# Sums over partitions of the adaLN vectors: VectorE block transposes and partials through DRAM in place of TensorE matmuls with a column of ones

## The chip, the cores and the metric

The kernel runs on one core of a Trainium2 chip. The metric is device time in microseconds (us) of that core, the median of several executions. All arithmetic is on float32 data; the large products are float32 split into a high and a low float32r part.

## The reference, cut to what matters

One encoder layer on x (1 x 1024 x 2048) with a conditioning vector c (1 x 2048). Everything that the change touches comes from the first line: a vector of 6144 sums over the 2048 rows of `w_ada`, cut into `shift`, `scale` and `gate`.

```python
mod = jax.nn.silu(c) @ w_ada + b_ada            # (1, 6144)
shift, scale, gate = jnp.split(mod, 3, axis=-1)
h = rmsnorm(x, pre_g) * (1.0 + scale[:, None]) + shift[:, None]
proj = h @ w_in                                  # q, k, v, gate_a, u, gate_p
...
g = jax.nn.sigmoid(h @ w_merge + b_merge)
merged = g_a * (y_a @ w_br_attn) + g_p * (y_p @ w_br_pool)
o = merged @ w_out
return x + gate[:, None] * rmsnorm(o, post_g)
```

`shift` and `scale` are wanted early for the first half of h's 2048 columns and later for the second half. `gate * post_g` is wanted only by the last stage, which multiplies every row of o with it.

## The kernel before, in words

The work is a chain of large products, each cut with Strassen's scheme (Winograd's form) into seven products (`product`, L233 to L238). One pair of output blocks is one call of `strassen`: seven products of 12 matmuls each (3 forms: high by high, high by low, low by high; 4 matmuls of 128x512 in each). TensorE works through these pairs with hardly a pause. For each product ScalarE makes the high part of the weights (`whi`, L96) and VectorE the low part (`wlo`, L97). Four buffers of each let them run ahead. VectorE also adds products that lie in PSUM to others (`u<-V,u`, L103), which frees the PSUM bank V of a pair for the next pair's product T3.

The modulation vector is made in three ways. The parts that are needed first (columns 0 to 3 of the first half) come from matmuls at the start of the program (`row_sums`, `modulation`). The late parts come from VectorE beside the first pass over the weights (`pass1`): `ada_sums(j)`, j = 4 to 7, and `gate_sum(kc, q)`, q = 0 and 1, each load rows of `w_ada` and accumulate them, weighted with silu(c), over the 16 groups of 128 rows into `accs[j]` (128x512) and `gacc[q]` (128x1024). What is then left is a sum over the 128 partitions. `sum_rows` does it by TensorE: the accumulator is the moving operand, and `onez` (128x32, a column of ones beside zeros) the weights; four such matmuls fill four groups of 32 rows of one PSUM bank.

- `late_rows` does it for the four `accs` (bank PMR, tile `msum`), `late_columns` turns the four rows into columns with four transposes on TensorE (bank PMT) and adds the bias into `modc`.
- `gate_row` does it for the two `gacc` (bank GATE), adds the bias, multiplies with post_g (both in `grow`, fetched by `gate_vectors` as rows), and stores 2048 numbers to `pg_d` in DRAM.

The order of this side work is written by hand. `units` holds 64 pairs of a load and a weighted sum; `unit_step(n)` runs load n and sum n - 3 (`AHEAD` = 3) and, by the table `then`, one further step ahead of sum m = n - 3. One `unit_step` comes after most products of a pair (`EASY`). Within an engine a layer below the kernel places the instructions by dependence; those in `keep(...)` stay in program order, and the others may be placed earlier. The loads and stores of the main work are on SP's queue, in order. GpSimd's queue (POOL) carries memsets that claim buffers, and a few DMAs.

At the start of the program, POOL fetches six small vectors (`rows`), then claims with one-column memsets the buffers `xT`, `B11h` and so on, which ScalarE and VectorE write before the first products (PB, L822). The first modulation columns are made at the same time: `GEMV` matmuls on eight tiles of `w_ada` that SP loads, the sums `PM`, and the first transposes of x (`XT`).

Of the kernel before, what the change touches and what calls it, by code (L numbers as in the profile page):

```python
# [21 lines left out]
P = 128  # L22
# [21 lines left out]
def encoder_layer(ctx: ExitStack, tc: tile.TileContext, x, c, table, w_ada, b_ada, pre_g,  # L44
# [32 lines left out]
    def uid(s):  # L77
        cnt[0] += 1
        return f"{s}_{cnt[0]}"

    def bank(tag, name="b"):
        return psum.tile([P, 512], F32, tag=tag, name=uid(name), bufs=1 if tag in SEEDED else 2)
# [8 lines left out]
    def keep(ins):  # L91

        return tc.keep_in_program_order(ins)
# [8 lines left out]
    def add(o, a, b, eng=None):  # L102
        return (eng or nc.vector).tensor_tensor(o, a, b, ALU.add)  # L103
# [30 lines left out]
    ws_d = {n: dram.tile([D // 2, D // 2], F32, name=f"ws_d{n}") for n in ("S1", "S2", "S3", "S4")}  # L134
    m_d = dram.tile([D, S], F32, name="m_d")
    pg_d = dram.tile([1, D], F32, name="pg_d")


    def put(op, name, j, src):
# [1011 lines left out]

        return load_, sum_

    onez = gp.tile([P, 32], F32, name="onez")
    nc.gpsimd.memset(onez, 0.0)
    nc.gpsimd.memset(onez[:, 0:1], 1.0)
    accs, gsum = {}, {}

    def bias_lines():
# [2 lines left out]

    def gate_vectors():

        gsum["v"] = t = xa.tile([P, 2, 512], F32, tag="xa", name=uid("grow"))
        nc.gpsimd.memset(t, 0.0)
        for k, src in enumerate((b_ada[0, 2 * D:3 * D], post_g[0])):
            for n in range(4):
                nc.gpsimd.dma_start(t[32 * n:32 * n + 1, k], src[n * 512:(n + 1) * 512].rearrange("(o n) -> o n", o=1))

    def sum_rows(name, srcs):

        ps = bank("at", name)
        for n, src in enumerate(srcs):
            nc.tensor.matmul(ps[32 * n:32 * n + 32, :], onez, src, start=True, stop=True, tile_position=(0, 32 * n))
        return ps

    def gate_row():
        t, g = (gsum["v"][:, k] for k in range(2))
        add(t, sum_rows("GATE", [gacc[q][:, n * 512:(n + 1) * 512] for q in range(2) for n in range(2)]), t)  # L1180
        nc.vector.tensor_tensor(t, t, g, ALU.mult)
        for k in range(4):
            nc.gpsimd.dma_start(pg_d[0:1, k * 512:(k + 1) * 512], t[32 * k:32 * k + 1, :])

    def late_rows():
        pm = sum_rows("PMR", [accs[j] for j in range(4, 8)])
        gsum["m"] = xa.tile([P, 1024], F32, tag="xa", name="msum")[:, 0:512]
        nc.scalar.activation(gsum["m"], pm, AF.Copy)

    def late_columns():  # L1190
        pt = bank("at", "PMT")
        for g in range(4):
            nc.tensor.transpose(pt[:, g * P:(g + 1) * P], gsum["m"][:, g * P:(g + 1) * P], ident)
        sums_ = pt.rearrange("p (g h j r) -> p g h j r", g=2, h=2, j=4)[:, :, :, :, 0]
        bias = cols[:, 16:48].rearrange("p (g j h) -> p g h j", g=2, h=2)[:, :, :, 4:8]
        for g in range(2):
            nc.vector.tensor_tensor(modc[:, g, :, 4:8], sums_[:, g], bias[:, g], ALU.add)
        nc.vector.scalar_tensor_tensor(
            modc[:, 1, :, 4:8], modc[:, 1, :, 4:8], 1.0,
            cols[:, 48:64].rearrange("p (j h) -> p h j", h=2)[:, :, 4:8], op0=ALU.add, op1=ALU.mult)  # L1200
# [3 lines left out]
    for j in range(4, 8):  # L1204
        units += ada_sums(j)
    nu = len(units)
    then = {nu: late_rows, nu + 2: late_columns, 6 - AHEAD: bias_lines, nu + 2 * KT - AHEAD: gate_vectors}
    units += [gate_sum(kc, q) for q in range(2) for kc in range(KT)]

    def unit_step(n):  # L1210
# [6 lines left out]
            units[n][0]()  # L1217

    side = deque(lambda n=n: unit_step(n) for n in range(len(units) + AHEAD))
    side.extend((lambda: None, gate_row))  # L1220
    EASY = ((0, 2, 4, 6), (0, 1, 3, 5, 6), (0, 2, 4, 6))
    n1 = PAIRS - RAMP - 9
    sums = deque(weight_sums(j, h_) for h_ in range(2) for j in range(KT // 2))
# [755 lines left out]
```

## Time and profile before

| | before |
|---|---|
| median of 3 runs | 2086.41 us (2085.77 to 2087.27) |
| the profiled execution | 2088.67 us, of which 2086.9 us are the span of the instructions |
| TensorE (PE) | 2070.1 us busy, 99% |
| VectorE (DVE) | 1556.7 us, 75% |
| ScalarE (ACT) | 1111.0 us, 53% |
| GpSimd (POOL) | 42.6 us, 2% |
| DMA | 476.62 MB, mean 228 GB/s |

Times in the profile count from the start of the span. A fp32 matmul is two passes in the records: the four matmuls of PMR are eight rows "x6" and "x2".

### The profile page before, as it was taken

The page shows a single profiled execution, that of the slowest core. Times are in us where ns is not written, and L with a number is a line of the kernel's source. Part 1 is how long each engine was busy: PE and PEld are TensorE (multiplying, and loading weights), DVE is VectorE, ACT ScalarE, POOL GpSimd, SP SyncE. Part 2 cuts the span into 40 slices and gives each one's busy share as a digit, 9 for nine tenths or more (in the row PEclk, how much of TensorE's full clock was granted, in tenths as well). Part 3 has the DMA queues.
Part 4 walks back from the last instruction along what each step waited for, and adds up shares of the span by engine and source line. Part 5 has one row for each costly group of instructions (what it writes and reads, how often), then busy time and mean ns, then how long its engine had stood idle before and what let it go on. Part 6 is the DMA issues. An engine that isn't in the chain of part 4 may idle for free.

```text
span 2086.9 us, 29056 instructions
## 1 busy us (share of the span) xinstructions
PE 2070.1 (99%) x9524; PEld 1702.2 (82%) x9524; DVE 1556.7 (75%) x2805; ACT 1111.0 (53%) x2121; POOL 42.6 (2%) x143
## 2 busy tenths in 40 slices
PE   8999999999999999999999999999999999999998
PEld 6678887888888888888888888888888788888886
DVE  5889677776565876777777688857867977889667
ACT  5764444444564634666665444334645644767554
POOL 1100000001000000000000000010000000000000
PEclk9999999999999999999999999999999999999999
DMA  9978877887675477645554576675754566786897
GB/s 343 355 270 267 282 240 245 282 284 223 198 232 170 156 250 258 208 164 174 182 170 149 186 233 222 208 239 187 232 175 158 176 201 202 225 305 207 297 334 247
DMA packets 303393, 476.62 MB, mean 228 GB/s; under 512 B 24322, under 2 KB 140650, under 8 KB 303240
## 3 DMA queue, kind: packets, MB, share of 16 engines
q1 hardware_dynamic: 297616, 459.89, 67.2%
q0 software_dynamic: 4560, 12.75, 1.6%
q10 hardware_dynamic: 1064, 2.11, 0.3%
q8 instruction: 75, 1.23, 0.3%
q14 instruction: 78, 0.64, 0.1%
HBM read 346.70 MB, written 130.05 MB: 228 GB/s over the span
## 4 chain that ended last, share of the span: by engine, by line
PE 91%; DMA 4%; DVE 3%; ACT 1%; issue 1%; SPq 0%; DVEq 0%; ACTq 0%; POOL 0%; POOLq 0%
PE Z L237 30%; PE V L237 20%; PE X L237 20%; PE Z L1686 2%; PE Z L1688 2%; PE Z L1687 2%; PE PB L822 1%; PE X L1686 1%; PE X L1687 1%; PE X L1688 1%; PE V L1687 1%; PE V L1686 1%; PE V L1688 1%; DMA raw<-in_w_in_dram 1%; PE PT L1396 1%
## 5 line engine op out<-in xcount | busy, mean ns | idle before, releaser
L96 ACT ACTIVATE whi<-raw 128x512 fp32r<-128x512 f32 (+1 forms) x528 | 314.7, 600 | 482.8 <-PE Z L237 235.2
L97 DVE TENSOR_TENSOR wlo<-raw,whi 128x512 fp32r<-128x512 f32 (+1 forms) x528 | 339.7, 649 | 144.5 <-PE Z L237 110.9
L97 DVE TENSOR_TENSOR wlo<-wr,whi 128x512 fp32r<-128x512 f32 x224 | 150.7, 689 | 51.5 <-ACT whi L96 46.0
L96 ACT ACTIVATE whi<-wr 128x512 fp32r<-128x512 f32 x224 | 138.2, 628 | 86.9 <-DVE wlo L97 29.8
L103 DVE TENSOR_TENSOR raw<-raw,raw 128x512 f32<-128x512 f32 x76 | 52.5, 690 | 92.7 <-DMA raw<-in_w_merge_dram 62.6
L96 ACT ACTIVATE whi<-ws 128x512 fp32r<-128x512 f32 (+1 forms) x88 | 53.0, 602 | 72.2 <-PE X L237 60.8
L237 PE MATMUL Z<-B22h,whi 128*128 128x512 f32 x328 | 89.9, 392 | 0.0
L237 PE MATMUL Z<-T2h,wlo 128*128 128x512 f32 x328 | 88.9, 390 | 0.8 <-DVE wlo L97 0.8
L237 PE MATMUL Z<-T1h,whi 128*128 128x512 f32 x328 | 89.6, 390 | 0.0
L237 PE MATMUL X<-B11h,whi 128*128 128x512 f32 x328 | 89.5, 391 | 0.0
L237 PE MATMUL X<-B21h,whi 128*128 128x512 f32 x328 | 89.5, 391 | 0.0
L237 PE MATMUL V<-T3h,whi 128*128 128x512 f32 x328 | 89.4, 391 | 0.0
L237 PE MATMUL V<-T4h,whi 128*128 128x512 f32 x328 | 89.3, 391 | 0.0
L237 PE MATMUL Z<-T2h,whi 128*128 128x512 f32 x328 | 89.0, 390 | 0.3 <-ACT Z L293 0.2
L237 PE MATMUL X<-B11l,whi 128*128 128x512 f32 x328 | 89.2, 390 | 0.0
L237 PE MATMUL Z<-T1l,whi 128*128 128x512 f32 x328 | 89.0, 390 | 0.0
L237 PE MATMUL Z<-B22l,whi 128*128 128x512 f32 x328 | 88.9, 390 | 0.0
L237 PE MATMUL V<-T3l,whi 128*128 128x512 f32 x328 | 88.9, 390 | 0.0
L237 PE MATMUL X<-B21l,whi 128*128 128x512 f32 x328 | 88.8, 390 | 0.0
L237 PE MATMUL V<-T4h,wlo 128*128 128x512 f32 x328 | 88.8, 390 | 0.0
L237 PE MATMUL X<-B11h,wlo 128*128 128x512 f32 x328 | 88.8, 390 | 0.0
L237 PE MATMUL V<-T4l,whi 128*128 128x512 f32 x328 | 88.8, 390 | 0.0
(421 smaller groups left out, 4908.7 us busy)
## 6 DMA issues: line engine op xcount, KB each, us to landing
part<-part_d SPq DMA_DIRECT2D x136, 256.0 KB, 5.0
ada<-in_w_ada_dram SPq DMA_DIRECT2D x128, 256.0 KB, 5.4
raw<-in_w_merge_dram SPq DMA_DIRECT2D x64, 512.0 KB, 5.4
wr<-ws_dS SPq DMA_DIRECT2D x60, 512.0 KB, 5.4
raw<-in_w_in_dram SPq DMA_DIRECT2D x56, 512.0 KB, 4.1
wr<-in_w_out_dram SPq DMA_DIRECT2D x48, 512.0 KB, 5.0
proj_d<-part SPq DMA_DIRECT2D x68, 256.0 KB, 2.3
sw<-in_w_out_dram SPq DMA_DIRECT2D x64, 256.0 KB, 4.9
```

What stands on the lines that cost most here:

```text
L96: ins = (nc.scalar.activation(hi, src, AF.Copy), nc.vector.tensor_tensor(lo, src, f32(hi), ALU.subtract))
L97: nc.vector.tensor_tensor(lo, src, f32(hi), ALU.subtract))
L103: return (eng or nc.vector).tensor_tensor(o, a, b, ALU.add)
L237: nc.tensor.matmul(ps, w_[:, i], op[mov][j][m_], start=fresh and i == 0 and n == 0, stop=i == nj - 1 and n == 2, skip_group_check=True)
L822: keep(nc.tensor.matmul(opened[i, blk], w[:, kh, nt * P:(nt + 1) * P], mov[kh][m], start=j == n == 0, stop=j == 1 and n == 5, skip_group_c ...
L1396: nc.tensor.transpose(pt[:, i * P:(i + 1) * P], p[:, i * P:(i + 1) * P], ident)
L1686: nc.tensor.matmul(pb, hi, w[0], start=first, stop=False, skip_group_check=True)
L1687: nc.tensor.matmul(pb, lo, w[0], start=False, stop=False, skip_group_check=True)
L1688: nc.tensor.matmul(pb, hi, w[1], start=False, stop=last, skip_group_check=True)
```

## The change

`sum_rows`, `late_rows` and `onez` go. Six calls of `fold` come: VectorE transposes an accumulator in blocks of 32x32, sums each block row over 32 numbers into a tile of 128x4x4 (or 128x4x8 for the gate), and a DMA on POOL's queue stores that to DRAM (`fold_d`). `fetch_folds` loads it back with four DMAs so that the four partials of one output lie in one partition, and `sum_folds` adds the four. `gate_row` now works on 128x16 columns; `gate_vectors` fetches b_ada and post_g in the same layout, number by number, into a tile of its own and without a memset, and the product goes to `pg_d` number by number in one DMA. `late_columns` comes two units later than before.

```diff
+    fold_d = {what: dram.tile([P, 64], F32, name=f"fold_{what}") for what in ("columns", "gate")}
...
-    onez = gp.tile([P, 32], F32, name="onez")
-    nc.gpsimd.memset(onez, 0.0)
-    nc.gpsimd.memset(onez[:, 0:1], 1.0)
...
     def gate_vectors():
 
-        gsum["v"] = t = xa.tile([P, 2, 512], F32, tag="xa", name=uid("grow"))
-        nc.gpsimd.memset(t, 0.0)
+        gsum["v"] = t = xa2.tile([P, 2, KT], F32, name="gate_vectors")
         for k, src in enumerate((b_ada[0, 2 * D:3 * D], post_g[0])):
-            for n in range(4):
-                nc.gpsimd.dma_start(t[32 * n:32 * n + 1, k], src[n * 512:(n + 1) * 512].rearrange("(o n) -> o n", o=1))
-
-    def sum_rows(name, srcs):
-
-        ps = bank("at", name)
-        for n, src in enumerate(srcs):
-            nc.tensor.matmul(ps[32 * n:32 * n + 32, :], onez, src, start=True, stop=True, tile_position=(0, 32 * n))
-        return ps
+            nc.gpsimd.dma_start(t[:, k], src.rearrange("(t n) -> n t", n=P))
+
+    def fold(what, src, t0):
+
+        w = src.shape[1]
+        nt = w // P
+        turned = xa.tile([P, 1024], F32, tag="xa", name=uid("turned"))[:, 0:w]
+        keep(nc.vector.transpose(turned, src))
+        r = xa2.tile([P, 4, 8], F32, tag="fold", name=uid("fold"), bufs=2)[:, :, 0:nt]
+        keep(nc.vector.tensor_reduce(r.rearrange("p u t -> p t u"), turned.rearrange("p (t u j) -> p t u j", u=4, j=32),
+                                     op=ALU.add, axis=AX.X))
+        nc.gpsimd.dma_start(fold_d[what].rearrange("p (u t) -> p u t", u=4)[:, :, t0:t0 + nt], r)
+
+    def fetch_folds(what):
+
+        gsum[what] = t = xa2.tile([P, 4, KT], F32, name=uid("folds"))
+        for u in range(4):
+            nc.gpsimd.dma_start(t[32 * u:32 * u + 32], fold_d[what].rearrange("(a i) c -> i a c", a=4)[:, :, u * KT:(u + 1) * KT])
+
+    def sum_folds(what):
+
+        t = xa2.tile([P, KT], F32, name=uid("sums"))
+        keep(nc.vector.tensor_reduce(t, gsum[what].rearrange("p a t -> p t a"), op=ALU.add, axis=AX.X))
+        return t
 
     def gate_row():
-        t, g = (gsum["v"][:, k] for k in range(2))
-        add(t, sum_rows("GATE", [gacc[q][:, n * 512:(n + 1) * 512] for q in range(2) for n in range(2)]), t)
+        t, (b, g) = sum_folds("gate"), (gsum["v"][:, k] for k in range(2))
+        add(t, t, b)
         nc.vector.tensor_tensor(t, t, g, ALU.mult)
-        for k in range(4):
-            nc.gpsimd.dma_start(pg_d[0:1, k * 512:(k + 1) * 512], t[32 * k:32 * k + 1, :])
-
-    def late_rows():
-        pm = sum_rows("PMR", [accs[j] for j in range(4, 8)])
-        gsum["m"] = xa.tile([P, 1024], F32, tag="xa", name="msum")[:, 0:512]
-        nc.scalar.activation(gsum["m"], pm, AF.Copy)
+        nc.gpsimd.dma_start(pg_d[0].rearrange("(t n) -> n t", n=P), t)
 
     def late_columns():
-        pt = bank("at", "PMT")
-        for g in range(4):
-            nc.tensor.transpose(pt[:, g * P:(g + 1) * P], gsum["m"][:, g * P:(g + 1) * P], ident)
-        sums_ = pt.rearrange("p (g h j r) -> p g h j r", g=2, h=2, j=4)[:, :, :, :, 0]
+        sums_ = sum_folds("columns").rearrange("p (j g h) -> p g h j", g=2, h=2)
...
-    then = {nu: late_rows, nu + 2: late_columns, 6 - AHEAD: bias_lines, nu + 2 * KT - AHEAD: gate_vectors}
+    then = {nu + 1: partial(fetch_folds, "columns"), nu + 4: late_columns, 6 - AHEAD: bias_lines,
+            nu + 2 * KT - AHEAD - 3: gate_vectors}
+    then.update({8 * (j - 3): lambda j=j: fold("columns", accs[j], 4 * (j - 4)) for j in range(4, 8)})
+    then[nu + KT] = lambda: fold("gate", gacc[0], 0)
...
-    side.extend((lambda: None, gate_row))
+    side.extend((lambda: fold("gate", gacc[1], 8), partial(fetch_folds, "gate"), lambda: None, gate_row))
```

On TensorE the order stays as it was, with the twelve instructions (8 matmuls with `onez`, 4 transposes) taken out. Three other places move.

POOL, at the start of the program, before the change: the memsets that claim buffers follow each other.

```order
L389 MEMSET shz 128x128
L398 MEMSET tab 33x8
L455 MEMSET rb 128x1
L435 MEMSET xT_187 128x1
L435 MEMSET xT_189 128x1
L435 MEMSET xT_191 128x1
```

POOL at the same place now:

```order
L390 MEMSET shz 128x128
L399 MEMSET tab 33x8
L456 MEMSET rb 128x1
L1165 DMA gate_vectors<-in_b_ada_dram 128x16x1
L1165 DMA gate_vectors<-in_post_norm_g_dram 128x16x1
L436 MEMSET xT_189 128x1
L436 MEMSET xT_191 128x1
```

The two element-by-element DMAs of `gate_vectors`, written for the end of `pass1`, have no wait and stand among the first instructions of POOL, ahead of all the memsets that claim xT, B11h and the rest.

DVE, behind the last weighted sum of `accs[7]`, before the change (`raw`, `ws` and `wlo` are the weights of the main products; `modc` the modulation columns; `gacc` the gate's accumulator; `u<-V,u` the addition that frees bank V):

```order
L106 TENSOR_TENSOR raw_3669<-raw_3669,raw_3667 128x4x128
L97 TENSOR_TENSOR wlo_3898<-raw_3669,whi_3897 128x512
L103 TENSOR_TENSOR raw_3839<-raw_3839,raw_3841 128x4x128
L97 TENSOR_TENSOR wlo_3916<-raw_3667,whi_3915 128x512
L97 TENSOR_TENSOR wlo_3942<-raw_3839,whi_3941 128x512
L106 TENSOR_TENSOR raw_3839<-raw_3839 128x4x128
L97 TENSOR_TENSOR wlo_3948<-ws_3945,whi_3947 128x512
L1197 TENSOR_TENSOR modc<-PMT_3886,cols 128x2x4 x2
L1198 SCALAR_TENSOR_TENSOR modc<-modc,cols 128x2x4
L612 SCALAR_TENSOR_TENSOR gacc_3798<-gada_3763,sc,gacc_3798 128x1024
L106 TENSOR_TENSOR ws_4110<-raw_4008 128x512
L103 TENSOR_TENSOR u_839_3864<-V_3767,u_839_3864 128x512
```

DVE at the same place now, from the reduction of the last block transpose on:

```order
L1174 TENSOR_REDUCE fold_3807<-turned_3805 128x4x4
L611 TENSOR_SCALAR gacc_3810<-gada_3707,sc 128x1024
L97 TENSOR_TENSOR wlo_3925<-raw_3681,whi_3924 128x512
L613 SCALAR_TENSOR_TENSOR gacc_3810<-gada_3749,sc,gacc_3810 128x1024
L103 TENSOR_TENSOR raw_3851<-raw_3851,raw_3853 128x4x128
L613 SCALAR_TENSOR_TENSOR gacc_3810<-gada_3777,sc,gacc_3810 128x1024
L97 TENSOR_TENSOR wlo_3951<-raw_3851,whi_3950 128x512
L106 TENSOR_TENSOR raw_3851<-raw_3851 128x4x128
L97 TENSOR_TENSOR wlo_3957<-ws_3954,whi_3956 128x512
L1187 TENSOR_REDUCE sums_3981<-folds_3855 128x16
L1200 TENSOR_TENSOR modc<-sums_3981,cols 128x2x4 x2
L1201 SCALAR_TENSOR_TENSOR modc<-modc,cols 128x2x4
```

The reduction `sums<-folds` stands in DVE's queue eight rows behind the fold whose way through DRAM it waits for; the addition `u<-V,u` of this pair is the very next row behind what is shown.

DVE at the end of the gate's sums, now (before the change the additions `grow<-GATE,grow` and the product stood at about this place):

```order
L1174 TENSOR_REDUCE fold_5050<-turned_5048 128x8x4
L97 TENSOR_TENSOR wlo_5104<-raw_4999,whi_5103 128x512
L103 TENSOR_TENSOR raw_4999<-raw_4999,raw_5001 128x4x128
L106 TENSOR_TENSOR raw_4999<-raw_4999 128x4x128
L97 TENSOR_TENSOR wlo_5110<-ws_5107,whi_5109 128x512
L106 TENSOR_TENSOR ws_5305<-raw_5164 128x512
L103 TENSOR_TENSOR u_1069_5022<-V_4941,u_1069_5022 128x512
L97 TENSOR_TENSOR wlo_5146<-raw_4844,whi_5145 128x512
L1187 TENSOR_REDUCE sums_5140<-folds_5095 128x16
L103 TENSOR_TENSOR sums_5140<-sums_5140,gate_vectors 128x16
L1193 TENSOR_TENSOR sums_5140<-sums_5140,gate_vectors 128x16
```

The same pattern: seven rows between the reduction that a DMA stores and the one that waits for the four loads.

## The prediction

> **What bounds the kernel now.** I read the page first, then the busy time by stage, then the order of time at the four places that the change touches. The page:
>
> ```profile
> span 2086.9 us, 29056 instructions
> PE 2070.1 (99%) x9524; PEld 1702.2 (82%) x9524; DVE 1556.7 (75%) x2805; ACT 1111.0 (53%) x2121; POOL 42.6 (2%) x143
> ...
> PE 91%; DMA 4%; DVE 3%; ACT 1%; issue 1%; SPq 0%; DVEq 0%; ACTq 0%; POOL 0%; POOLq 0%
> ...
> L237 PE MATMUL Z<-T2h,wlo 128*128 128x512 f32 x328 | 88.9, 390 | 0.8 <-DVE wlo L97 0.8
> ```
>
> TensorE is the bound: it is busy in 99% of the span and makes 91% of the chain. The last row says how far the others are behind it: in the whole run it waited 0.8 us for a low weight of VectorE. By stage (PE, weight loads, DVE, ACT, POOL, then the granted clock and the share of the DMA engines):
>
> ```profile
> 0.00:20.00 20.00, 14.63 (x72) 7.34 (x73) 6.61 (x15) 5.66 (x10) 4.92 (x38) 1.00 0.92 300
> 20.00:40.00 20.00, 19.47 (x120) 15.51 (x119) 13.71 (x33) 16.72 (x39) 0.00 (x0) 1.00 1.04 364
> 219.00:360.00 141.00, 140.77 (x621) 114.66 (x619) 107.42 (x165) 57.82 (x95) 0.00 (x0) 1.00 0.77 251
> 435.00:520.00 85.00, 85.00 (x379) 69.46 (x378) 61.52 (x85) 35.71 (x58) 6.72 (x13) 1.00 0.78 252
> ```
>
> Two things follow. In the stage with the side work (219 to 520) PE is full and DVE has a quarter to spare, so what leaves PE there is time won. In the first 20 us PE is busy 14.63 only, and the DMA engines are the full resource (0.92, then 1.04): what is added to them there is paid.
>
> **What leaves TensorE.** PE in order of time at the four places (start, length, tile, count):
>
> ```profile
> 353.10 1.07 PE L237 MATMUL X<-B11h,wlo 128*128 128x512 f32 x4
> 354.10 1.06 PE L1175 MATMUL PMR<-acc,onez 128*32 128x512 f32 x6
> ...
> 356.12 1.08 PE L237 MATMUL V<-T3l,whi 128*128 128x512 f32 x4
> ...
> 357.95 0.84 PE L237 MATMUL Z<-B22h,whi 128*128 128x512 f32 x3
> 359.01 1.05 PE L1175 MATMUL PMR<-acc,onez 128*32 128x512 f32 x2 [0.23 <-DVE acc L612]
> ...
> 361.25 1.07 PE L237 MATMUL Z<-B22h,wlo 128*128 128x512 f32 x4
> 362.17 1.07 PE L237 MATMUL Z<-T2h,whi 128*128 128x512 f32 x4
> ...
> 366.70 1.07 PE L237 MATMUL X<-B21h,wlo 128*128 128x512 f32 x4
> 367.61 0.60 PE L1193 MATMUL PMT<-ident,msum 128*128 128x128 f32 x4
> ...
> 368.98 1.08 PE L237 MATMUL V<-T4l,whi 128*128 128x512 f32 x4
> ```
>
> ```profile
> 506.11 1.07 PE L237 MATMUL Z<-T1h,wlo 128*128 128x512 f32 x4
> 507.10 1.06 PE L1175 MATMUL GATE<-gacc,onez 128*32 128x512 f32 x8
> ...
> 509.13 1.08 PE L237 MATMUL X<-B11l,whi 128*128 128x512 f32 x4
> ```
>
> The lengths overlap, so the price is read from starts. From 362.17 to 366.70 lie five groups of four: 0.906 us each. Two groups are 1.81 us; what is over between the rows above belongs to the removed work, its restart and its 0.23 us of waiting included. First PMR: 356.12 - 353.10 = 3.02, over 1.21. Second PMR: 361.25 - 357.95 = 3.30, over 1.49. PMT: 368.98 - 366.70 = 2.28, over 0.47. GATE: 509.13 - 506.11 = 3.02, over 1.21. The four matmuls of one bank fill four column groups side by side, which is why eight passes of about 600 ns cost little more than one. **Sum: 4.4 us off the path**, 0.21% of the kernel. That is the whole gain. The ACT copy into `msum` goes too; ACT is half idle, so it counts as nothing.
>
> **What is added to VectorE, and what hides it.** No row shows a block transpose. The nearest are a cast at 0.43 us and a two-operand instruction at 0.69 us for 128x512, and 1.28 us for 128x1024:
>
> ```profile
> 12.80 0.43 DVE L803 CAST whi<-wide 128x512 fp32r<-128x512 f32 x1
> 13.26 0.69 DVE L106 TENSOR_TENSOR wlo<-wide,whi 128x512 fp32r<-128x512 f32 x1
> L612 DVE SCALAR_TENSOR_TENSOR gacc<-gada,sc,gacc 128x1024 f32<-128x1024 f32 x30 | 38.4, 1280 | 1.7 <-DMA gada<-in_w_ada_dram 1.5
> ```
>
> I take 0.69 and 1.28 for transpose and reduction alike (one pass over one element stream; at twice that a transpose would be 1.4 and 2.6). Four column folds are 4 x 1.38 = 5.5 us, two gate folds 2 x 2.56 = 5.1; the two `grow` instructions (1.4) go. That is 9 us more, 5.5 of it in a stage with 33 us of idle DVE. DVE's idle time there is mostly waiting for PE to give `wlo` buffers back, so it runs ahead; I cost it at nothing. If it were not ahead, the most is one fold, 1.4 or 2.6 us, at each of six places.
>
> **The way through DRAM.** `sums<-folds` waits on DVE, with all of DVE's queue behind it, for: a store, four issues, a load. The prices:
>
> ```profile
> L1183 POOL DMA_DIRECT2D pg_d<-grow x4: 484/484/487, 510.2 to 511.6; - x4
> ...
> DMA to landing us min/median/max: 2.2/3.2/4.9
> 358.21 0.75 DVE L612 SCALAR_TENSOR_TENSOR acc<-ada,sc,acc 128x512 f32<-128x512 f32 x1
> 371.49 0.68 DVE L103 TENSOR_TENSOR u<-V,u 128x512 f32<-128x512 f32 x1
> 376.26 1.07 PE L237 MATMUL V<-T3h,whi 128*128 128x512 f32 x4
> 508.10 1.20 PE L237 MATMUL X<-B11h,whi 128*128 128x512 f32 x4
> ```
>
> *Columns.* The last weighted sum ends at 358.96. Transpose, one `wlo`, reduction: 361.0. Store 3.2, three issues of 0.48 ahead of the last load, load 3.2: 368.9 (366.9 with the fastest landings, 372.3 with the slowest). Seven rows of DVE work lie between, so DVE waits about a microsecond, up to 4. Behind it comes `u<-V,u`, done 1.3 us after the landing: 370.2, at most 373.6. PE wants bank V for its next T3 product at 376.26, less the 3.2 us that PMR and PMT took: 373.1. So it fits by 3 us, and misses by 0.5 at worst; I take 0.2. *Gate.* The same way ends 8 us after its reduction. DVE waits some 3 us there, but the next `wlo` behind it is for the product T2, whose last third starts eleven groups (10 us) behind the row at 508.10: covered.
>
> **What is added at the start.** The order shows the two `gate_vectors` DMAs as the first work of POOL behind `rb`. Each moves 2048 single numbers.
>
> ```profile
> 4.75 0.12 POOL L455 MEMSET rb<- 128x1 f32 x1
> 4.98 0.12 POOL L657 MEMSET B11h<- 128x1 f32 x1
> 8.13 0.38 SPq L761 DMA_DIRECT2D wide<-in_w_in_dram  x1
> 10.20 1.03 PE L528 MATMUL GEMV<-ada,scz 128*32 128x256 f32 x8
> 13.00 0.69 ACT L684 ACTIVATE B11h<-XT,modc 128x512 fp32r<-128x512 f32 x1 [1.34 <-PE XT L491]
> PEld GEMV L528 <- DMA ada<-in_w_ada_dram: 4.7, 6, 1.2
> ...
> L381 POOL DMA_DIRECT2D rows<-in_pre_norm_g_dram x1: 492/492/492, 3.1 to 3.1; - x1
> L837 POOL DMA_DIRECT2D ramp_d<-c x8: 539/539/579, 49.8 to 74.7; - x8
> ...
> q0 software_dynamic: 256, 0.02, 1.2%
> ```
>
> *POOL's time.* An issue of 16 rows took 492 ns, one of 128 rows 539: 0.42 ns for a row more. Carried on to 2048 it is 1.35 us for each DMA, 2.7 for both. The memset of B11h moves from 4.98 to 7.7; ACT writes B11h at 13.0. Nothing is lost as long as one issue takes less than 4 us.
>
> *The DMA engines' time.* The last row is POOL's queue in the 14 us from 476 to 490: 256 packets (half of them 128 bytes, half semaphore writes) took 1.2% of 16 engines, 10.5 ns each. 4096 numbers at that price are 43 us of engine time, 2.7 us on each of 16. Below, the packets could fall in gaps (0). The loads that they meet are the tail of the `ada` tiles, for which GEMV waits six times, then x, then `wide`, issued at 8.13 and cast at 12.80 for the first product. All of it is just in time, and the engines are full, so most of it is paid: I take 2.0 us. Nothing behind gives it back, since PE is full from 20 us on.
>
> Here the Trainium skill speaks against the change: "DMA: Bandwidth & Descriptors", rules for kernel authors, says that a strided last dimension becomes one descriptor per element and should be rearranged. "VectorE: DVE Perf Modes", the three transpose paths, puts such an element-wise copy at 19 times a 1309 ns transfer of 128x128; that is an estimate of 1.5 ns per element, 6.2 us for 4096, and by it the sum would be 2088.4. No row of this trace shows such a copy.
>
> The other small DMAs (2048 numbers of `pg_d`, six stores of 512 short runs, eight loads of 128) come at 300 us and later, where the DMA engines have a fifth free and nobody waits; nothing.
>
> **The sum.** -4.4 (PE) + 2.0 (start) + 0.2 (bank V) = -2.2 us. The profiled execution has a span of 2086.9 and a time of 2088.67, 2.3 above the median of 2086.41; the terms are differences, so I apply them to the median: **2084.2 us**. 0.2%, 4.2 us, is about what a measurement here can tell from no change, so this is "the same", slightly below.
>
> **Rivals.**
> - *The start is free.* The numbers slip in between the loads. For: POOL's six small DMAs ahead of them do. Against: the DMA share of 0.92 and the six waits of GEMV. Time: 2086.4 - 4.4 = 2082.0, faster.
> - *POOL is slow at making 2048 descriptors.* Then the memsets are late and the first products with them. It decides from 4 us per issue on; beyond it the start slips by twice the excess. At 8 us the start is 8 us late: 2086.4 - 4.4 + 8 + 2 = 2092, slower. For: no DMA here has over 128 rows, so the slope is carried on 16-fold. Against: the slope itself.
> - *A number costs the DMA engines far more than a short row.* In the window from 1 to 13 us the hardware queue's packets, mostly 1 KB rows, took 52 ns each:
>
> ```profile
> q1 hardware_dynamic: 3329, 3.45, 89.6%
> ```
>
>   That bounds it above: 13.2 us on each engine, 2095. Half-way in ratio, 23 ns, it is 6.0 us and 2088.2. The skill's 19 times comes to the same place.
> - *The way through DRAM holds PE.* If landings take 5 us and more under load, bank V is late by 1 to 3 us: 2085 to 2087.
>
> **How the numbers follow.** Forecast 0.50; start free 0.18; POOL slow 0.13; dear numbers 0.11; DRAM way 0.08. Faster by over 0.2% (below 2082.2): the second case and a little of the first, 0.20. Slower (above 2090.6): POOL slow, and a third of the dear numbers, 0.17. The same: 0.63. The range runs from 2081.6, the full gain with the spread of the runs, to 2089.5, which takes in the half-way price of the numbers and leaves out slow POOL and the upper bound.
>
> **What would show it.** PE loses L1175 and L1193, and its starts around them close up. DVE gets nine microseconds more busy time and two waits for `folds` of 1 to 4 us, with no wait of PE for bank V behind. The two L1165 issues take about 1.35 us each; the first product PB starts at 15.5 to 16 in place of 13.74. The prediction is wrong if PB starts at 13.8 (then 2082), or if B11h waits for POOL.

## The result and the profile after

The changed kernel takes 2098.22 us, the median of 6 runs (2096.37 to 2099.54); the kernel before took 2086.84 beside it (2085.70 to 2090.41). The ratio is 1.0047, 95% interval 1.0036 to 1.0058: 10 us slower by the ratio, 11.4 by the two medians, and outside the forecast range of 2081.6 to 2089.5. The profiled executions say the same, 2097.8 us of span against 2086.9.

The page of the changed kernel; its lines are numbered one higher than before in `product` (L238 for L237):

```profile
span 2097.8 us, 29039 instructions
PE 2069.1 (99%) x9504; PEld 1701.9 (81%) x9504; DVE 1563.4 (75%) x2819; ACT 1111.1 (53%) x2120; POOL 48.0 (2%) x145
...
PE 85%; DMA 6%; DVE 4%; issue 3%; ACT 1%; SPq 0%; POOL 0%; DVEq 0%; ACTq 0%; POOLq 0%
...
L238 PE MATMUL V<-T3h,whi 128*128 128x512 f32 x328 | 89.8, 393 | 6.3 <-DVE u L103 6.3
L238 PE MATMUL Z<-T2h,wlo 128*128 128x512 f32 x328 | 89.1, 391 | 3.8 <-DVE wlo L97 3.8
```

TensorE's share of the chain fell from 91% to 85%, and in the last two rows stands what it now waits for: 6.3 us for `u` and 3.8 us for low weights, where the largest such entry before was 0.8. By stage (the columns as in the prediction):

```profile
0.00:20.00 20.00, 12.58 (x58) 6.12 (x59) 4.64 (x12) 3.79 (x7) 7.31 (x40) 0.91 0.95 260
360.00:390.00 30.00, 28.28 (x125) 23.06 (x125) 19.54 (x30) 12.22 (x20) 2.93 (x5) 1.00 0.81 257
435.00:470.00 35.00, 32.17 (x141) 25.97 (x140) 27.87 (x37) 14.16 (x23) 0.72 (x1) 1.00 0.84 273
500.00:520.00 20.00, 18.25 (x81) 14.80 (x80) 12.86 (x18) 7.36 (x12) 2.32 (x4) 1.00 0.70 223
520.00:540.00 20.00, 18.56 (x82) 14.90 (x81) 8.17 (x15) 7.10 (x13) 1.79 (x3) 1.00 0.63 69
```

Before, PE was full (30.00, 35.00, 20.00, 20.00) in the last four. The places are these, in order of time (PE rows with the wait ahead of them in brackets):

```profile
378.26 1.20 PE L238 MATMUL V<-T3h,whi 128*128 128x512 f32 x4 [1.72 <-DVE u L103]
...
437.12 1.20 PE L238 MATMUL V<-T3h,whi 128*128 128x512 f32 x4 [1.22 <-DVE u L103]
...
458.06 1.21 PE L238 MATMUL V<-T3h,whi 128*128 128x512 f32 x4 [1.61 <-DVE u L103]
...
517.27 1.19 PE L238 MATMUL V<-T3h,whi 128*128 128x512 f32 x4 [1.75 <-DVE u L103]
...
526.26 1.20 PE L238 MATMUL Z<-T2h,wlo 128*128 128x512 f32 x4 [1.44 <-DVE wlo L97]
...
546.92 1.19 PE L238 MATMUL Z<-T2h,wlo 128*128 128x512 f32 x4 [1.23 <-DVE wlo L97]
...
596.77 1.20 PE L238 MATMUL Z<-T1h,whi 128*128 128x512 f32 x4 [0.58 <-ACT u L252]
...
600.43 1.20 PE L238 MATMUL X<-B11h,whi 128*128 128x512 f32 x4 [0.62 <-ACT c L333]
```

To see what each costs, every matmul of one trace is set beside the same matmul of the other and the starts are subtracted. The changed kernel runs 3.3 us late at 60 us of the time before, 0.1 at 371 (so PMR and PMT did give 3.2), 3.7 at 440, 5.6 at 475, 8.2 at 520, 11.5 at 620, and 10.6 at the end. That is the ledger which the experiments have to explain.

*The columns' way through DRAM* (POOL rows are DMA issues; the bracket is what the engine waited for):

```profile
362.49 0.68 DVE L1174 TENSOR_REDUCE fold<-turned 128x16 f32<-128x512 f32 x1
363.46 0.71 POOL L1176 DMA_DIRECT2D fold_columns<-fold  x1 [37.97 <-DVE fold L1174]
370.88 2.22 POOL L1182 DMA_DIRECT2D folds<-fold_columns  x4 [6.71 <-DMA fold_columns<-fold]
376.86 0.26 DVE L1187 TENSOR_REDUCE sums<-folds 128x16 f32<-128x64 f32 x1 [7.52 <-DMA folds<-fold_columns]
377.52 0.68 DVE L103 TENSOR_TENSOR u<-V,u 128x512 f32<-128x512 f32 x1
378.23 0.33 SPq L338 DMA_DIRECT2D part_d<-u  x1
378.83 0.38 SPq L188 DMA_DIRECT2D raw<-in_w_merge_dram  x1
```

From the end of the reduction (363.2) to the sums it took 13.7 us; DVE stood 7.52 us, `u` came late, and with it SP: its next load of `raw` stands behind the store of `u` in the same queue. *The gate's store* writes 2048 single numbers, each a run of four bytes by itself. What it does is seen in the DMA throughput of 520 to 540 us (one figure per half microsecond) and in the landings (KB each, median us):

```profile
GB/s 225 258 328 326 119 78 62 16 0 0 0 0 0 0 0 6 64 345 50 16 1 1 13 8 17 26 43 41 61 29 25 29 8 25 20 8 51 109 139 201
...
raw<-in_w_merge_dram SPq DMA_DIRECT2D x2, 512.0 KB, 14.6
...
pg_d<-sums POOLq DMA_DIRECT2D x1, 8.0 KB, 13.0
```

The store of 2048 numbers is issued at 525.90. From 529 to 538.5 the DMA engines move 1 to 61 GB/s, with two loads of half a megabyte waiting; those land after 14.6 us. In the same stretch before, `raw` landed in 5.0 us.

### The profile page after: what moved, and what is told of

Its sections match the earlier page's. It is cut to its first block, busy times and chain, and to the rows that moved or that the text cites. A ratio compares the mean times of both kernels' runs of the same rounds, so it can differ in the third digit from the quotient of the medians.

```text
span 2097.8 us, 29039 instructions
## 1 busy us (share of the span) xinstructions
PE 2069.1 (99%) x9504; PEld 1701.9 (81%) x9504; DVE 1563.4 (75%) x2819; ACT 1111.1 (53%) x2120; POOL 48.0 (2%) x145
## 3 DMA queue, kind: packets, MB, share of 16 engines
q8 instruction: 74, 1.21, 0.2%
## 4 chain that ended last, share of the span: by engine, by line
PE 85%; DMA 6%; DVE 4%; issue 3%; ACT 1%; SPq 0%; POOL 0%; DVEq 0%; ACTq 0%; POOLq 0%
PE Z L238 27%; PE X L238 18%; PE V L238 18%; PE Z L1692 2%; PE Z L1693 2%; PE Z L1694 2%; PE PB L823 2%; DMA raw<-in_w_merge_dram 2%; PE X L1692 1%; PE V L1692 1%; PE V L1693 1%; PE X L1693 1%; PE V L1694 1%; PE X L1694 1%; PE PT L1402 1%
## 5 line engine op out<-in xcount | busy, mean ns | idle before, releaser
L106 DVE TENSOR_TENSOR ws<-raw 128x512 f32<-128x512 f32 (+1 forms) x88 | 57.5, 653 | 55.1 <-DMA raw<-in_w_merge_dram 42.3
L238 PE MATMUL V<-T3h,whi 128*128 128x512 f32 x328 | 89.8, 393 | 6.3 <-DVE u L103 6.3
L238 PE MATMUL Z<-T2h,wlo 128*128 128x512 f32 x328 | 89.1, 391 | 3.8 <-DVE wlo L97 3.8
L238 PE MATMUL Z<-T1h,whi 128*128 128x512 f32 x328 | 89.7, 390 | 0.6 <-ACT u L252 0.6
L238 PE MATMUL X<-B11h,whi 128*128 128x512 f32 x328 | 89.5, 391 | 0.6 <-ACT c L333 0.6
L238 PE MATMUL Z<-B22h,whi 128*128 128x512 f32 x328 | 89.6, 392 | 0.0
L238 PE MATMUL X<-B21h,whi 128*128 128x512 f32 x328 | 89.5, 391 | 0.0
L238 PE MATMUL Z<-T2h,whi 128*128 128x512 f32 x328 | 89.0, 390 | 0.3 <-ACT Z L294 0.2
L238 PE MATMUL X<-B11l,whi 128*128 128x512 f32 x328 | 89.3, 390 | 0.0
L238 PE MATMUL V<-T4h,whi 128*128 128x512 f32 x328 | 89.2, 391 | 0.0
L238 PE MATMUL Z<-B22l,whi 128*128 128x512 f32 x328 | 88.9, 390 | 0.0
L238 PE MATMUL V<-T3l,whi 128*128 128x512 f32 x328 | 88.9, 390 | 0.0
L238 PE MATMUL Z<-T1l,whi 128*128 128x512 f32 x328 | 88.9, 389 | 0.0
L238 PE MATMUL X<-B21l,whi 128*128 128x512 f32 x328 | 88.9, 390 | 0.0
L238 PE MATMUL X<-B11h,wlo 128*128 128x512 f32 x328 | 88.8, 390 | 0.0
L238 PE MATMUL V<-T4h,wlo 128*128 128x512 f32 x328 | 88.8, 390 | 0.0
```

Of the source, the lines that this page charges most:

```text
L106: return nc.vector.tensor_tensor(o, a, b, ALU.subtract)
L238: nc.tensor.matmul(ps, w_[:, i], op[mov][j][m_], start=fresh and i == 0 and n == 0, stop=i == nj - 1 and n == 2, skip_group_check=True)
```

## The experiments

All ratios are to runs of the kernel before on the same chip. The lateness is that of the same matmul against the trace of before, in us, at six times of before and at the end; it is worked out as above from one profiled execution each (median over seven neighbours). Steps of up to 1.6 us stand also where nothing was changed: f4 is the kernel before up to 511 us, and it goes from -0.5 at 60 to 1.1 at 371.

| kernel | ratio, 95% interval | 60 | 371 | 440 | 475 | 520 | 620 | 2075 |
|---|---|---|---|---|---|---|---|---|
| changed | 1.0047 (1.0036 to 1.0058) | 3.3 | 0.1 | 3.7 | 5.6 | 8.2 | 11.5 | 10.6 |
| e1_vectors_late | 1.0045 (1.0032 to 1.0058) | 0.0 | -2.9 | 0.5 | 2.5 | 3.3 | 7.3 | 14.7 |
| e2_lag | 1.0025 (1.0014 to 1.0036) | 3.7 | 2.1 | 3.0 | 4.8 | 3.7 | 7.5 | 8.0 |
| e3_folds_only | 1.0000 (0.9991 to 1.0009) | -0.6 | 0.3 | 0.1 | 1.2 | 1.2 | 1.2 | 0.2 |
| e4_columns_only | 1.0022 (1.0012 to 1.0032) | -0.4 | -2.9 | 3.6 | 3.6 | 3.6 | 3.6 | 3.3 |
| e5_store_runs | 1.0033 (1.0021 to 1.0045) | 4.3 | 1.1 | 5.1 | 7.6 | 7.1 | 7.0 | 7.4 |
| e6_no_singles | 1.0026 (1.0016 to 1.0036) | -0.1 | -1.8 | 1.9 | 3.9 | 4.3 | 4.3 | 3.4 |
| e7_long_runs_lag | 0.9996 (0.9987 to 1.0005) | -0.5 | -3.4 | -3.6 | -2.5 | -3.6 | -3.6 | -2.4 |
| e8_singles_on_before | 0.9996 (0.9987 to 1.0005) | -0.3 | -0.2 | -0.4 | -0.4 | -0.4 | -0.5 | -0.7 |
| f1_long_runs_no_lag | 1.0016 (1.0007 to 1.0024) | 2.8 | 0.1 | 2.1 | 3.4 | 4.9 | 4.9 | 3.0 |
| f2_vectors_at_start | 1.0013 (1.0003 to 1.0023) | 4.3 | 1.4 | 1.2 | 2.8 | 3.1 | 3.1 | 6.1 |
| f3_singles_store | 1.0030 (1.0018 to 1.0041) | 2.8 | -0.4 | -0.6 | 0.7 | 0.6 | 5.4 | 4.6 |
| f4_singles_later_on_before | 1.0025 (1.0014 to 1.0036) | -0.5 | 1.1 | 1.1 | 1.1 | 1.1 | 4.9 | 3.8 |

**Is it DVE's work or the way through DRAM?** e3 puts the six folds on DVE into the kernel before, with no store:

```diff
+        keep(nc.vector.transpose(turned, src))
+        keep(nc.vector.tensor_reduce(r..., op=ALU.add, axis=AX.X))
     # before, called for accs[4..7] and gacc[0..1]; sum_rows stays
```

> The kernel before (2086.8), with its sums on TensorE, and beside them the six block transposes and six row sums on DVE into tiles that nobody reads; no partials go through DRAM. The turned tiles take xa buffers as in the changed kernel. Theory A (the blocked queue): DVE has room, the time is that of before within 1 us, 2086 to 2088. Theory B (the added DVE work or the xa buffer): most of the 12 us of waits that the changed kernel shows is here too, 2092 to 2097. Between them: the waits at 458 and 512 us, which follow the folds of the gate and no landing, are here, about 1.7 us each, 2090.

Measured 1.0000. The 11 us of work are hidden but for 1.1 us behind the first gate fold (0.1 at 440, 1.2 at 475), and in this trace that is given back by the end. Theory B, in which the work itself is dear, falls. e2 keeps everything and takes the sums later:

```diff
-    then = {nu + 1: partial(fetch_folds, "columns"), nu + 4: late_columns, ...
+    then = {nu + 1: partial(fetch_folds, "columns"), nu + 10: late_columns, ...
-    side.extend((..., partial(fetch_folds, "gate"), lambda: None, gate_row))
+    side.extend((..., partial(fetch_folds, "gate"), lambda: None, lambda: None, lambda: None, lambda: None, gate_row))
```

> The changed kernel with the two sums of the partials taken later: late_columns six units of side work later, gate_row three units later. The same instructions on every engine. Theory A (DVE's queue stands blocked behind the landing of the partials, 7.5 and 7.1 us, and the work behind it, u and the loads that SP issues behind u's store, comes late): the jumps of PE at 378, 437, 526, 546 and 586 to 589 us go, 1.85 + 1.67 + 1.74 + 1.52 + 1.84 = 8.6 us; 2089.6, with no idle time of DVE in front of the sums. Theory B (it is the work added to DVE, 9 us, or the xa buffer that the turned tile takes, in a loop of DVE, SP and loads that had no slack): the time stays within 1.5 us of the changed kernel's 2098.2, the waits for the partials gone or not.

Measured 1.0025, between the two. The columns' step went as theory A has it: 371 to 440 costs 0.9 in place of 3.6, and 475 to 520 gains 1.1 in place of losing 2.6. But 520 to 620 still costs 3.8. So A holds for the two waits of DVE, not for what follows 525 us. e4 does the columns alone the new way:

```diff
-    then[nu + KT] = lambda: fold("gate", gacc[0], 0)
+    # gate_row, gate_vectors, sum_rows, onez as in the kernel before
```

> The changed kernel with the gate done as before (rows on four partitions, eight matmuls with the onez tile, its vectors loaded late into an xa buffer): only the columns are summed by DVE and through DRAM. From the aligned starts: the removed PMR and PMT give 3.2 us, the waits of PE at 378 and 437 us take 1.85 + 1.67 = 3.5, the start costs nothing; 2087.1, with the same wait of 7 us of DVE for the partials. If the lateness of SP's loads that this wait leaves goes on through the next stage (the waits at 458 and 512 us), 2089 to 2091. If the waits of the changed kernel come from the gate alone, 2083.6.

Measured 1.0022, 4.6 us over before in place of 0.3, and not by the second way either: nothing is lost from 440 to 620. From 371 to 440 it lost 6.5 us, not 3.5, since one wait there grew to 2.46 us and TensorE then ran at half its pace. PE's rows, and the stages around (the column behind POOL is the granted clock):

```profile
435.43 1.81 PE L238 MATMUL V<-T3h,whi 128*128 128x512 f32 x4 [2.46 <-DVE u L103]
437.04 1.91 PE L238 MATMUL V<-T3l,whi 128*128 128x512 f32 x4
438.74 1.30 PE L238 MATMUL V<-T3h,wlo 128*128 128x512 f32 x4
439.88 1.08 PE L238 MATMUL Z<-B22h,whi 128*128 128x512 f32 x4
```

```profile
430.00:435.00 5.00, 2.97 (x14) 2.12 (x12) 0.91 (x2) 1.87 (x4) 0.00 (x0) 1.00 0.87 300
435.00:440.00 5.00, 4.57 (x13) 3.64 (x14) 4.96 (x8) 0.63 (x1) 0.00 (x0) 0.66 0.76 215
```

Starts 1.6 and 1.7 us apart in place of 0.9: the wait of 2.46 us cost 4 us.

**The single numbers.** e5 turns the finished gate once more on DVE and stores it in runs of 128 bytes:

```diff
-        nc.gpsimd.dma_start(pg_d[0].rearrange("(t n) -> n t", n=P), t)
+        keep(nc.vector.transpose(sq[:, 1], sq[:, 0]))
+        for a in range(4):
+            nc.gpsimd.dma_start(pg_d[0].rearrange("(t a j) -> a t j", a=4, j=32)[a], sq[32 * a:32 * a + KT, 1])
```

> The changed kernel with one thing else: the finished gate, 128x16, is turned once more by DVE and stored to pg_d as 64 runs of 128 bytes, in place of 2048 single numbers. (The two landing tiles of the partials share one buffer, for room.) Theory C (the store of single numbers holds the DMA engines: in the changed kernel they moved 320 GB/s before it, some 30 for 9 us behind it, and raw landed 14.6 us after its issue there, 5.0 before the change): the jumps of PE at 546 and 586 to 589 us go, 1.52 + 1.84 = 3.4 us; some 7 us over the kernel before, raw lands in 5 to 7 us in the stage 520 to 540, and DVE's longest wait for raw is under 5 us (10.0 in the changed kernel). Theory A (the wait of DVE for the partials makes the loads late there): nothing changes, 10 to 11 us over before.

Measured 1.0033, as theory C has it (7 us over before): nothing is lost from 520 to 620, `raw` lands in 5.7 us from 520 to 540, and the longest wait of DVE for it from 520 to 620 is 3.1 us (10.0 in the changed kernel). e6 takes the single numbers of the vectors away too:

```diff
-            nc.gpsimd.dma_start(t[:, k], src.rearrange("(t n) -> n t", n=P))
+            for a in range(4):
+                keep(nc.gpsimd.dma_start(t[32 * a:32 * a + KT, k], src.rearrange("(t a j) -> a t j", a=4, j=32)[a]))
```

> As the one with the turned store, and the gate's vectors too are loaded as 128 runs of 128 bytes, late, and no single numbers at the start: the gate is finished in the turned layout. Theory C, with the start worth its 3.3 us: 11 - 3.4 - 3.3, 4 to 5 us over before, with the remaining waits of PE at 376, 433, 453, 511 and 518 us. If an earlier start only meets later loads again, as in the run that moved the vectors alone (no gain in the time): 7 us over before.

Measured 1.0026, 5.4 us over before: between the two expectations by the time. Its trace has the start back and keeps it to the end (4.4 us earlier than e5 at 60, 4.0 at 2075). e1 moves the vectors alone:

```diff
-            nc.gpsimd.dma_start(t[:, k], src.rearrange("(t n) -> n t", n=P))
+            keep(nc.gpsimd.dma_start(t[:, k], src.rearrange("(t n) -> n t", n=P)))   # fold's store too: behind it in order
```

> The changed kernel with one thing moved: the two element-wise loads of the gate vectors stand on POOL's queue behind the four column stores, at about 430 us, and no longer at the start. Everything else, the order of every other engine too, is as in the changed kernel (2098.2). If the start costs what the aligned starts of the two traces show (the steady run of PB products is 3.3 us late, 1.2 us of it through a granted clock of 0.91 in the first 20 us), this kernel is 3.3 us faster: 2094.9, with the first PB back at 13.7 to 13.9 us and a clock of 1.00 in the first stage. Rival: the lateness of the start is eaten up later, since the loads of the ramp come no earlier; then it gains less than 1 us, 2097.5 or more.

Measured 1.0045: no gain in the time. In the trace the start is 3.3 us earlier, as expected, and stays so to 520, but behind it come a new wait at 855 us and longer ones at 543 and 1661 (2.24 and 1.84 us for 1.23 and 1.10), each followed by half pace. The places at 855 and 1661 lie far from anything that was changed, and the profiled execution is the slowest of the five (2103.60 us, the median is 2099.80). With intervals of 2.7 and 2.3 us on either side this pair cannot tell 3.3 from 0; f2 below is the better test.

e8 adds the gate's store of single numbers to the kernel before, right behind its own:

```diff
+        nc.gpsimd.dma_start(singles_d[0].rearrange("(t n) -> n t", n=P), numbers)   # in gate_row, issued at 511.7
```

> The kernel before, and behind its four stores of pg_d one more: 2048 single numbers, 128x16, to a row of DRAM that nobody reads. Theory C: the DMA engines move under 60 GB/s for some 9 us behind it, the raw loads of that time land in 12 to 15 us in place of 5, DVE waits for one of them by 5 us or more, and PE gets waits of 2 to 4 us between 515 and 600 us: 2 to 4 us over before. Theory A: a transfer that nobody waits for costs nothing: 0 within 0.5 us.

The DMA engines did what theory C says, for 13 us even, up to 525 (500 to 520 us, the store issued at 511.67):

```profile
GB/s 248 289 287 309 352 375 393 406 369 111 57 303 246 102 137 250 324 221 346 311 98 45 105 179 12 0 0 8 7 1 0 0 0 25 12 4 12 0 8 8
...
raw<-in_w_merge_dram SPq DMA_DIRECT2D x3, 512.0 KB, 13.3
...
singles_d<-numbers POOLq DMA_DIRECT2D x1, 8.0 KB, 14.4
```

DVE waits 6.1 us for one of these loads. Yet the time is 0.9996, and from 505 to 640 us PE waits nowhere. So the stall is real and its price is not fixed. Two readings were left: the kernel before has its loads further ahead, or the place is a harmless one. f4 tells them apart; it has the same store in the same kernel 19 us later:

```diff
-    side.extend((lambda: None, gate_row))
+    side.extend((lambda: None, gate_row, lambda: None, lambda: None, lambda: None, lambda: None, singles))
```

> The kernel before with the same extra store of 2048 single numbers, to a row that nobody reads, issued four units of side work later: at some 530 us, where the combined kernel with this store had it (there it took 4.7 us of PE's time), and no longer at 511.7, where it cost the kernel before nothing. If the place decides (behind 525 us come the loads of sw, raw and xt that fill the DMA engines), this kernel loses 3 to 5 us, 1.0015 to 1.0025 of before, with a wait of PE of 1.5 to 2 us around 570 and half pace behind it. If the lead of the loads decides, and the kernel before has it everywhere: 0 within 1 us.

Measured 1.0025, 5.2 us: the place decides. The one wait that was expected, of 1.5 to 2 us with half pace behind it, did not come; there are three shorter ones. PE's rows with waits (the store is issued at 530.34; the kernel before has none of them):

```profile
573.88 1.20 PE L238 MATMUL V<-T3h,whi 128*128 128x512 f32 x4 [0.83 <-DVE u L103]
...
590.11 1.20 PE L238 MATMUL Z<-T1h,whi 128*128 128x512 f32 x4 [1.41 <-ACT u L252]
...
593.76 1.20 PE L238 MATMUL X<-B11h,whi 128*128 128x512 f32 x4 [0.61 <-ACT c L333]
```

What differs between the two places stands in the stages of before (last two columns: the DMA engines' share, GB/s). It fits that a store at 511.7 stalls a stretch with room behind it, and one at 530 the loads of the next; no run varies the load of the DMA engines by itself.

```profile
520.00:540.00 20.00, 20.00 (x89) 16.41 (x88) 9.59 (x15) 9.74 (x16) 0.00 (x0) 1.00 0.44 140
540.00:620.00 80.00, 80.00 (x387) 66.86 (x386) 46.95 (x76) 54.12 (x135) 0.00 (x0) 1.00 0.75 240
```

**Everything mended, and each fault put back.** e7 has no single numbers, one store for each sum in 128 runs of 256 bytes, and the lag:

```diff
-        r = xa2.tile([P, 4, 8], F32, tag="fold", ...)[:, :, 0:nt]        # six stores of 512 short runs
+        r = gsum["r" + what][:, :, t0:t0 + nt]                           # one tile and one store for each sum
+        if t0 + nt == KT:
+            keep(nc.gpsimd.dma_start(fold_d[what].rearrange("p (u t) -> p u t", u=4), gsum["r" + what]))
```

> Everything together: no single numbers, the gate's vectors late, one store of the partials for each sum (128 runs of 256 bytes in place of four and two stores of 512 runs of 16 and 32 bytes), and the sums six and three units of side work later. If the waits come from small pieces in the DMA engines and from DVE's queue behind the landing, none is left, and the 4.1 us that TensorE is relieved of show, less up to 1 us for the folds on DVE: 1 to 4 us under the kernel before. If the added work on DVE and the smaller number of free xa buffers matter by themselves, 0 to 4 us over before.

Measured 0.9996 (0.9987 to 1.0005): against the changed kernel's 1.0047 nearly all is mended, against the kernel before nothing can be told. Its trace shows the removed matmuls: 3.6 us early at 520 and 620. By 2075 it is 2.4. f1 takes the lag away again:

```diff
-    then = {..., nu + 10: late_columns, ...            # and the three more lambdas ahead of gate_row
+    then = {..., nu + 4: late_columns, ...
```

> The combined kernel (0.9996 of before) without the lag: the sums of the partials stand again where the changed kernel has them. The store is still one of 128 runs of 256 bytes; it landed in 3.9 us for the columns and 7.9 for the gate, where the 512 short runs took up to 9.1. Theory A (DVE's queue blocked behind the landing is paid): DVE waits 2 to 4 us for the columns and 3 to 6 for the gate, and PE loses 3 to 6 us against the combined kernel, with waits for u or wlo behind both sums; 1 to 4 us over before. If the short runs were the whole trouble: as the combined kernel, 0.9996, no wait of PE behind the sums.

Measured 1.0016. DVE waits 5.3 us for the columns (7.5 with the short runs; the store now takes 3.7 us after its issue, not 6.7), and 371 to 440 costs 2.0, where e7 loses nothing. So both count: the short runs and the missing lag. f2 puts the single numbers at the start back into e7:

```diff
+        gsum["v"] = t = xa2.tile([P, 2, KT], F32, name="gate_vectors")
+        for k, src in enumerate((b_ada[0, 2 * D:3 * D], post_g[0])):
+            nc.gpsimd.dma_start(t[:, k], src.rearrange("(t n) -> n t", n=P))
```

> The combined kernel with the gate's vectors loaded as in the changed kernel, 4096 single numbers at the start. If the start is paid to the end: the first PB at 15.4 to 16 us in place of 13.7, the clock of the first 20 us under 1.00, the steady run 3.3 to 4 us later, and 3.3 to 4 us more in the end: 1.0013 of before, 2 us over it. If a late start is eaten up by later waits: as the combined kernel within 1 us.

Measured 1.0013, the number expected: 1.7 thousandths above e7, 3.5 us, and with the two intervals some 1 to 6. The first PB is at 15.89. f3 puts the gate's single-number store into e7 (with one more turn of the gate on DVE), issued at 531.25:

```diff
+        nc.gpsimd.dma_start(pg_d[0].rearrange("(t n) -> n t", n=P), sq[:, 0, 0:KT])
```

> The combined kernel with pg_d stored as in the changed kernel, 2048 single numbers in one store. The DMA engines will move under 60 GB/s for some 9 us behind it either way. If its price depends on the lead of the loads (none in the changed kernel, which had been made late by two blocked sums, some in the kernel before, where it cost nothing): as the combined kernel within 1 us. If the store has a price of its own in this place: 2 to 3.4 us more, 1.001 of before.

Measured 1.0030. It loses 4.8 us from 520 to 620, more than either expectation, with a wait of 1.90 us at 574 and half pace behind it. (Its trace also has a start 2.8 us late, which the edit does not touch.)

Read down the column from 520 to 620: every kernel with the single-number store issued after 520 us loses 3.3 to 4.8 us there (the changed one, e1, e2, f3, f4); every other loses nothing. From 371 to 440: those with DVE waiting for the columns lose 2.0 to 6.5, those with the lag 0.9 at most. The gate's sums show in the wait of PE for `wlo` behind them, at 526 us in the changed kernel: it is there in the five kernels in which DVE waits for the gate's partials (0.41 us in e5, 0.85 in e1, 0.95 in e6, 1.44 in the changed one, 1.57 in f1), and in none with the lag.

## Why the prediction was wrong, point by point

- *What leaves TensorE, 4.4 us.* Right. PMR and PMT gave 3.2 (60 to 371, in the changed kernel), the removed GATE 1.1 (475 to 520 in e2 and e7, where nothing waits there): 4.3.
- *What is added to VectorE, nothing.* Right in its durations (transposes 0.71 and 1.24 us, reductions 0.68 and 1.21) and nearly so in the sum: e3 is 1.0000. But the folds are not free at every place: behind the first gate fold 1.1 us are lost in e3, and 1.9 in the changed kernel, where its store comes with it.
- *The way through DRAM, columns: 0.2 us, 0.5 at worst.* **This step failed.** The prices were those of `pg_d` stores, four of 512 contiguous numbers, and of `grow` loads. A store of 512 runs of 16 bytes took 6.7 us behind its issue (3.2 taken, 4.9 at worst), each issue 0.556 (0.484), the loads 5.0. DVE waited 7.5 us, not 1 (eight rows of its work lay between, not seven), and PE lost 2.3 us at once and 3.6 by 440. The second part was not seen at all: SP's queue is in order, so a late `u` makes the next `raw` late. It is issued at 378.83, 6.0 us later than before; the loads of `raw` behind it come 6.6, 6.7, 5.9, 5.4 and 3.5 us late, while PE itself was 2.4 late. The last of these, at 430.35, is the one for which DVE stood 3.52 us, until 435.8, with `u` and PE's wait at 437 behind it. The row that should have warned is in the trace of before. PE was full, but with nothing to spare, which neither its share of 99% nor its 0.8 us of waiting for low weights shows:

```profile
432.70 0.69 DVE L103 TENSOR_TENSOR u<-V,u 128x512 f32<-128x512 f32 x1
433.44 0.76 PEld L237 LDWEIGHTS V<-T3h,whi 128*128 128x128 f32 x4 [0.32 <-DVE u L103]
```

  The weight load for bank V came 0.05 us after `u`. "Fits by 3 us" was worked out at one use of bank V (376), not at those that follow.
- *The gate's way: covered by eleven groups.* Failed by the same price: DVE waited 7.1 us, not 3. From 475 to 520 the changed kernel loses 2.6 us, where the removed GATE gives e2 and e7 1.1. But only one of its two waits of PE there, the one at 526 (1.7 us in the ledger), follows the sums. The one at 517 (1.8 us) stands ahead of them: DVE had waited for `raw` until 515.9, behind the second gate fold, and two kernels with the lag have that wait too (f2 1.22 us, f3 0.90). What makes `raw` late there is open. DVE's rows:

```profile
515.92 0.69 DVE L106 TENSOR_TENSOR ws<-raw 128x512 f32<-128x512 f32 x1 [4.92 <-DMA raw<-in_w_merge_dram]
...
524.93 0.26 DVE L1187 TENSOR_REDUCE sums<-folds 128x16 f32<-128x64 f32 x1 [7.11 <-DMA folds<-fold_gate]
```

- *"The other small DMAs ... nobody waits; nothing."* **This step failed too**, by 3.3 us here and 3.8 to 4.8 in e2, f3 and f4. Nobody waits for `pg_d`, but behind its store the DMA engines moved next to nothing for 9.5 us, and the loads that they held up had somebody waiting.
- *The start, 2.0 us.* The mechanism was right, and the size of the first step: the first PB came at 15.62 (15.5 to 16 was said), the issues took 1.22 and 1.17 us (1.35), and throughput fell for three microseconds. In 0 to 20 us, the changed kernel:

```profile
GB/s 0 0 0 53 196 337 362 266 245 284 305 284 268 268 238 317 268 341 379 336 177 81 119 102 91 142 229 338 377 385 389 377 375 369 359 350 346 348 352 344
```

  Before, it was 318 to 381 in those slices, from 10 us on. What was missed is that TensorE, kept waiting for x, then ran slower: 3.3 us in all by the trace. By the times of the three pairs that differ in it (changed and e1, e5 and e6, e7 and f2) it is 0.4, 1.5 and 3.5 us, each uncertain by some 3 us. The granted clock is 0.50 from 16.4 to 19.8 us. Each of the four traces with the single numbers at the start has such a stretch, of 3.4 or 6.8 us, between 13.7 and 21.5 us; none of the ten others has one there. XT's waits and the PB rows behind them, 0.43 us apart where 0.23 is the pace:

```profile
12.87 0.44 PE L492 MATMUL XT<-ident,xt 128*128 128x128 f32 x2 [0.52 <-DMA xt<-in_x_dram]
13.96 0.81 PE L492 MATMUL XT<-ident,xt 128*128 128x128 f32 x4 [0.66 <-DMA xt<-in_x_dram]
15.62 0.47 PE L823 MATMUL PB<-B11h,whi 128*128 128x512 f32 x1 [0.85 <-DVE whi L804]
...
16.86 0.63 PE L823 MATMUL PB<-B21h,whi 128*128 128x512 f32 x1
17.29 0.63 PE L823 MATMUL PB<-B11h,wlo 128*128 128x512 f32 x1
```

- *The rivals.* The one that came nearest was "the way through DRAM holds PE", with chance 0.08; its price of 1 to 3 us was for one bank V, and it was held against the whole gain. POOL was not slow, and the numbers loaded at the start were not dear.

In one sum, from the ledger of the changed kernel: start +3.3, PMR and PMT -3.2, the columns' way +3.6, first gate fold and its store +1.9, the second gate fold and the gate's way less the removed GATE +2.6, the single-number store +3.3, -0.9 behind it: 10.6.

## What to carry to other kernels

A fully busy engine does not show how close its inputs come. Before putting a wait into an in-order queue, look at the next several uses of everything behind it, the DMA queue that those instructions feed included, and give a result that goes through DRAM as much lead as store and load have taken in rows of the same run length. A transfer that nobody waits for still has a price, paid by the loads behind it and set by its place: write to DRAM in long runs (one turn on VectorE made 128-byte runs of single numbers), or put the store where the DMA engines have room.

## What the runs showed of the hardware that was not expected

- *Single numbers cost far more to write than to read.* 4096 numbers loaded at the start took the throughput down from some 350 to 81 to 177 GB/s for 3 us, about 2.2 us of full rate lost: 0.5 ns for a number. 2048 numbers stored took it to 61 GB/s and less for 9.5 us, 4.6 ns for a number, and for 13 us in e8. The prediction's 10.5 ns over 16 engines (0.66) was near for the loads and was not applied to the store. What the engines do in the stall is not seen: in e8 the store's 8 KB are recorded as 32 packets of 256 bytes, all over by 515 us, and from 515 to 523 the trace records 27 packets, all of SP's queue, at 7 GB/s. The Trainium skill, in "DMA: Bandwidth & Descriptors", the specifications, says that transfers under 512 B are done as read-modify-write; the runs agree in that writes are the dear side, but no run here shows the mechanism.
- *A short wait can halve TensorE's pace.* Behind the start, the 14 traces have 33 waits of PE of 1.0 to 1.76 us, and none changed the pace. Six were longer: 1.81 us (f2 at 850), 1.90 (f3 at 574), 2.46 (e4 at 435), and 1.84, 2.24 and 2.67 in e1. Each was followed by two to three slow groups of four matmuls, up to 1.9 us apart in place of 0.91, with a granted clock of 0.66 over five microseconds in e4 and f3 (0.50 for 3.4 us): 1.4 to 1.7 us more. The Trainium skill's "TensorE: Matmul & The Clock Gate", Part 1, tells of a free-running activity window of about 3.4 us and of half the clock after an idle one; the length of the slow stretch, 3.4 us, agrees, while the idle time that was enough here is little more than half of that window.
- *Full clock can come late at the start.* In f1 and f3, without a single number at the start and without a wait for x, the pace is halved from PM to the first PB products all the same (first PB at 14.89 and 15.09, 2.8 us late at 60). In these two the trace's record of the granted clock begins only at 19.2 and 19.0 us, with full clock, and there the slow pace ends; in the twelve others it begins between 7.6 and 11.3 us. (A stage row of f1 or f3 reads 1.00 up to there, since it counts recorded drops alone.) So this is another case than the four with single numbers, which have full clock first and then lose it. Why the clock came late in these two is open, and 2.8 us of the lateness of f1 and f3 do not come from their edits.
